# A weight cast placed by TensorE's progress in the piece three ahead

## The chip, the cores and the metric

The kernel runs on one core of a Trainium2 chip. The metric is the device time of one execution in microseconds (us). The core's engines work side by side, each through its own list of instructions in order, and wait for one another by semaphores: TensorE (PE) multiplies, VectorE (DVE) and ScalarE (ACT) work element by element, GpSimd (POOL) helps with a few, and SyncE (SP) issues the fetches of weights.

## What is computed

Two layers of a decoder trunk, on 272 positions (16 learned meta positions and a sequence of 256) and a model width of 1024, all in 32-bit floating point. The reference, cut to its frame:

```python
for l in range(DEPTH):
    h = rms_norm(x, norm1_g[l])
    u = h @ w_in[l]
    (u_conv, c_q, c_kv, k_rope, hq, hf, hi, hg, u_gate) = jnp.split(u, SPLIT_POINTS, axis=-1)
    y_a = conv_module(u_conv, ...)      # causal depthwise conv of 31 taps, layer norm, projection
    y_b = mla(c_q, c_kv, k_rope, ...)   # 8 heads of latent attention, causal softmax, projection
    y_c = hgrn2(hq, hf, hi, hg, ...)    # gated linear recurrence, 4 heads, projection
    gates = jax.nn.sigmoid(u_gate).reshape(B, L, N_BRANCH, D)
    mix = gates[:, :, 0] * y_a + gates[:, :, 1] * y_b + gates[:, :, 2] * y_c
    x = x + mix @ w_out[l]
    h2 = rms_norm(x, norm2_g[l])
    x = x + jnp.square(jax.nn.relu(h2 @ w_ff1[l])) @ w_ff2[l]
return x[:, N_META:]
```

## The kernel before

All activations lie with channels on the 128 partitions and positions along the row. The dense weights are cut into 276 pieces of 128 x 1024 numbers, and `piece` (L206) brings one in: `fetch` issues its DMA on SP into one of three buffers `wraw`, ACT casts it to the matmul type as `whi` (L211), and DVE subtracts this from the raw piece to get the remainder `wlo` (L213). `whi` and `wlo` have four buffers each, so a cast overwrites the piece four back and must wait until PE has read that. A product is made of three matmuls, `mm3` (L220): high by high (L221), low by high (L222) and high by low (L223). A piece feeds eight such triples, 24 matmuls, for one accumulator `acc` (or `hx`) in PSUM. There are two `acc` buffers; ACT or DVE copies the finished one out, which frees it.

A layer has a mixer part and a feed-forward part. In the mixer part a list `dense` (L1012) holds the tiles of `w_in` (`head_tile`, L400, whose results `take`, L410, copies out), the gates (`gate_tile`, L980) and the projections of the three branches (`merge_tile`, L986). Between these the loop at L1023 takes steps of four streams: latent projections, HGRN2, attention, conv. The first merge tile needs the output `ys` of attention, so whatever is left of attention then runs with no other dense work to place: this is called attention's tail below.

The names in the tail: `mx` is a product of queries and keys in PSUM, `pr` its exp (L652), which ACT scales by the row's sum (L658, and for the 16 meta positions as `pm`, L657); `pt` is `pr` transposed by PE (L671) and `pts` its copy (L681); `sm` is the product with the values (L694, L701), and `ybhi` its cast (L217), which the merge tiles multiply by. HGRN2's own tail stands there too: `at`, `atm` and `atx` (L849, L863, L869) are its masked score blocks, `vtok` and `vmeta` (L883, L885) its values, transposed by PE (L879, L881) and multiplied with (L899 to L907). Before that HGRN2 takes an Ln of its decay on ACT in two halves, `lf` (L744), DVE scans each (L746), and ACT takes exponentials `ep` and `en` (L773, L774). `sg` (L417) is a tanh of an accumulator, with the copy at L419 beside it. Where a function is not in ACT's loaded table, the program has an ACT_TABLE_LOAD ahead of it. The conv's taps are multiply-adds on DVE (`cacc`, L939), and PE takes its mean over channels afterwards (`mx`, L947).

The order of each engine's list is set before the run by a scheduler that plays the program through in modelled time: of the instructions that could start it takes the one of highest priority. `tc.high_priority(offset=AHEAD)` raises fetch, cast and subtraction of a piece by 500 places, and so they are placed about as soon as a buffer is free. Semaphores are then added where data need them.

Of the kernel before, what the change touches and what calls it, by code (L numbers as in the profile page):

```python
# [35 lines left out]
FF = 4 * D  # L36
KF = FF // P
AHEAD = 500
NGATE = 15
NLAT = 8  # L40
BRANCHES = (1, 2, 0)
# [45 lines left out]
def block_kernel(ctx, tc, xT_d, pp_d, cc_d, win_d, wuq_d, wukv_d, wbr_d, wout_d, wff1_d, wff2_d, out_d):  # L87
    nc = tc.nc
    pe, act, dve, pool = nc.tensor, nc.scalar, nc.vector, nc.gpsimd
# [14 lines left out]
    def fetch(src, n=1024):  # L104
        raw = wsp.tile([P, 1024], F32, name="wraw", tag="wraw")
        nc.sync.dma_start(out=raw[:, :n], in_=src[:, :n])
        return raw

    xT = resid.tile([P, KD, L], F32, name="xT")
    pp = const.tile([P, DEPTH, NPP], F32, name="pp")  # L110
    with tc.high_priority(offset=2 * AHEAD):
        nc.scalar.dma_start(out=pp, in_=pp_d)
# [88 lines left out]
    def psum_sm():  # L201
        return ps_sm.tile([P, 512], F32, name="sm", tag="sm")

    newest = {}

    def piece(src, raw=None):  # L206

        with tc.high_priority(offset=AHEAD):
            raw = raw or fetch(src)
            hi = wsp.tile([P, 1024], F32R, name="whi", tag="whi", bufs=4)  # L210
            act.copy(out=hi, in_=raw)  # L211
            lo = wsp.tile([P, 1024], F32R, name="wlo", tag="wlo", bufs=4)
            newest["lo"] = dve.tensor_tensor(out=lo, in0=raw, in1=hi.bitcast(F32), op=SUB).ins  # L213
        return hi, lo
# [3 lines left out]
        dve.tensor_tensor(out=lo, in0=src, in1=hi.bitcast(F32), op=SUB)  # L218

    def mm3(out, whi, wlo, xhi, xlo, start, stop):  # L220
        pe.matmul(out, whi, xhi, start=start, stop=False)  # L221
        pe.matmul(out, wlo, xhi, start=False, stop=False)  # L222
        pe.matmul(out, whi, xlo, start=False, stop=stop)  # L223

# [84 lines left out]
    for l in range(DEPTH):  # L309
# [25 lines left out]
        t4 = t4p.__enter__()  # L335
        gpool = tc.tile_pool(name=f"gates{l}", bufs=NGATE)
        gp = gpool.__enter__()
# [31 lines left out]
        def win_acc(j, n0):  # L369
            hi, lo = piece(win_d[l, j], first["kv"] if l == 0 and j == 1 else None)  # L370
            xh, xl = xg if j < NLAT else (hhi, hlo)
            ps = psum_hx() if j < NLAT and j % 2 == 0 else psum_acc()
            for k in range(KD):
                o = k * P
                mm3(ps[:, :L - n0], hi[:, o:o + P], lo[:, o:o + P], xh[:, k, n0:], xl[:, k, n0:],
                    k == 0, k == KD - 1)
            return ps
# [10 lines left out]
        def rope_keys(j):  # L388

            with tc.high_priority(offset=AHEAD):  # L390
                raw = first["kr"] if l == 0 else fetch(win_d[l, j], KD * ROPE)
# [57 lines left out]
        def latent_steps():  # L449
# [44 lines left out]
            for g in range(2):  # L494
                uqhi, uqlo = piece(wuq_d[l, g])
                for h in range(4):
                    ps = psum_mx()[:, :L]
                    for j in range(2):
                        o = j * 512 + h * P
                        mm3(ps, uqhi[:, o:o + P], uqlo[:, o:o + P], cqhi[:, j, :], cqlo[:, j, :], j == 0, j == 1)  # L500
                    act.activation(out=msq_[:QK, h, :], in_=ps[:QK], func=AF.Square)
                    dve.tensor_tensor(out=qT[g][:, h, :], in0=ps, in1=csg, op=MUL)
                    yield
                with together():
                    for h in (3, 2, 1, 0):
                        pe.matmul(sums[32 * h:32 * h + 32, :L], sel96[:QK, g, :], msq_[:QK, h, :], start=(g == 0), stop=(g == 1))
                yield
# [3 lines left out]
            for w in qtiles:  # L511
# [10 lines left out]
                                     in1=heads(ra[:, 1, q0:3]), op0=MUL, op1=MUL)  # L522

            ukhi, uklo = piece(wukv_d[l])
            kT = [unit(f"kT{g}") for g in range(2)]
            vv = [half(f"vv{w}", "vv", 3) for w in range(3)]
# [459 lines left out]
        def merge_tile(i):  # L986
            b, m = divmod(i, KD)
            yh, yl = ys[BRANCHES[b]]
            if i == 0:
                mix["sum"] = [unit(f"mix{j}") for j in range(2)]  # L990
            if i % 2 == 0:
                mix["w"] = piece(wbr_d[l, i // 2])
            bhi, blo = mix["w"]
            ps = (psum_acc, psum_hx, psum_hx)[b]()
            for k in range(4):
                o = (i % 2 * 4 + k) * P
                mm3(ps[:, :N], bhi[:, o:o + P], blo[:, o:o + P], yh[:, k, T0:], yl[:, k, T0:], k == 0, k == 3)
            g, total = gates[i], mix["sum"][m // 4][:, m % 4, :N]
            with tc.high_priority(offset=AHEAD):
                dve.scalar_tensor_tensor(out=total if b == 0 else g[:, :N], in0=g[:, :N], scalar=1.0, in1=ps[:, :N], op0=ADD, op1=MUL)  # L1000
            if b > 0:
                dve.tensor_tensor(out=total, in0=total, in1=g[:, :N], op=ADD)
            if b == 2:
                if m == 0:
                    mix["hi"] = actp.tile([P, KD, L], F32R, name="mhi", tag="ahi")
                    mix["lo"] = actp.tile([P, KD, L], F32R, name="mlo", tag="alo")
                act.activation(out=mix["hi"][:, m, T0:], in_=total, func=AF.Copy, scale=0.5)
                dve.scalar_tensor_tensor(out=mix["lo"][:, m, T0:], in0=total, scalar=0.5, in1=mix["hi"][:, m, T0:].bitcast(F32),
                                         op0=MUL, op1=SUB)


        dense = [(head_tile, j) for j in range(NLAT, N_HEAD_TILES)] + [(gate_tile, i) for i in range(NGATE)]  # L1012
        for i in range(3 * KD):
            dense.append((merge_tile, i))
            if i + NGATE < 3 * KD:
                dense.append((gate_tile, i + NGATE))
        head_index = {(t[0], t[1]): j - NLAT for j, t in enumerate(tiles)}
# [26 lines left out]
        xhi = actp.tile([P, KD, L], F32R, name="xhi", tag="ahi")  # L1044
# [165 lines left out]
```

## Time and profile before

| | us |
|---|---|
| median of 3 runs | 954.34 (954.14 to 955.79) |
| the profiled execution | 952.41 |
| its span in the trace | 950.6 |
| PE busy | 927.6 |
| DVE busy | 714.1 |
| ACT busy | 525.0 |
| POOL busy | 55.7 |

The trace is of the profiled execution. Its span runs from the first recorded instruction to the last, and 1.8 us of the execution lie around it. Busy time of an engine leaves out waits and the issue of DMAs. A matmul's end is modelled, so the distance between two starts tells more of PE than a duration. In a timeline an entry stands for one instruction or a few alike in a row (x2), and the square brackets hold the idle time of that engine just before it and what ended it.

### The profile page before, as it was taken

The page shows a single profiled execution, that of the slowest core. Times are in us where ns is not written, and L with a number is a line of the kernel's source. Part 1 is how long each engine was busy: PE and PEld are TensorE (multiplying, and loading weights), DVE is VectorE, ACT ScalarE, POOL GpSimd, SP SyncE. Part 2 cuts the span into 40 slices and gives each one's busy share as a digit, 9 for nine tenths or more (in the row PEclk, how much of TensorE's full clock was granted, in tenths as well). Part 3 has the DMA queues.
Part 4 walks back from the last instruction along what each step waited for, and adds up shares of the span by engine and source line. Part 5 has one row for each costly group of instructions (what it writes and reads, how often), then busy time and mean ns, then how long its engine had stood idle before and what let it go on. Part 6 is the DMA issues. An engine that isn't in the chain of part 4 may idle for free.

```text
span 950.6 us, 18626 instructions
## 1 busy us (share of the span) xinstructions
PE 927.6 (98%) x7474; PEld 892.0 (94%) x7474; DVE 714.1 (75%) x1348; ACT 525.0 (55%) x945; POOL 55.7 (6%) x87
## 2 busy tenths in 40 slices
PE   7999999899999999999999999999999999999998
PEld 5899999879999999999999889998799999999998
DVE  7789999986887766555557799999869886675552
ACT  7567665644546555544445587666345566654331
POOL 4004100011000000000010021000100000000000
PEclk9999999999999999999999999999999999999999
DMA  8454433324545655555545444344145565555651
GB/s 267 132 178 136 154 112 129 117 66 134 175 137 180 197 177 174 171 174 173 177 159 174 137 132 158 113 153 123 60 153 182 169 193 191 191 186 186 204 198 56
DMA packets 42422, 149.16 MB, mean 157 GB/s; under 512 B 4704, under 2 KB 6368, under 8 KB 42336
## 3 DMA queue, kind: packets, MB, share of 16 engines
q1 hardware_dynamic: 40608, 146.10, 47.9%
q10 hardware_dynamic: 1728, 1.88, 0.6%
q8 instruction: 58, 0.95, 0.4%
q14 instruction: 28, 0.23, 0.1%
HBM read 146.91 MB, written 1.05 MB: 156 GB/s over the span
## 4 chain that ended last, share of the span: by engine, by line
PE 90%; DVE 4%; ACT 3%; issue 2%; DMA 1%; SPq 0%; ACTq 0%
PE acc L221 18%; PE acc L222 17%; PE acc L223 17%; PE hx L221 9%; PE hx L223 9%; PE hx L222 9%; DVE wlo L213 2%; PE mx L636 1%; PE hx L812 1%; ACT whi L211 1%; PE sm L694 1%; DMA xT<-in_xT_dram 1%; PE pt L671 1%; PE sm L701 0%; PE mx L221 0%
## 5 line engine op out<-in xcount | busy, mean ns | idle before, releaser
L211 ACT CAST whi<-wraw 128x1024 fp32r<-128x1024 f32 x276 | 289.5, 1050 | 339.0 <-PE acc L223 182.2
L213 DVE TENSOR_TENSOR wlo<-wraw,whi 128x1024 fp32r<-128x1024 f32 x276 | 337.3, 1223 | 156.4 <-ACT whi L211 155.3
L221 PE MATMUL acc<-hhi,whi 128*128 128x272 f32 (+1 forms) x704 | 206.0, 293 | 2.6 <-ACT scrahi L419 1.9
L223 PE MATMUL acc<-hlo,whi 128*128 128x272 f32 (+1 forms) x704 | 202.6, 288 | 0.2 <-DVE hlo L218 0.2
L222 PE MATMUL acc<-hhi,wlo 128*128 128x272 f32 (+1 forms) x704 | 201.9, 287 | 0.0
L221 PEld LDWEIGHTS acc<-hhi,whi 128*128 128x128 f32 x704 | 132.6, 188 | 7.5 <-ACT scrahi L419 2.1
L223 PEld LDWEIGHTS acc<-hlo,whi 128*128 128x128 f32 x704 | 132.3, 188 | 2.0 <-DVE hlo L218 0.6
L222 PEld LDWEIGHTS acc<-hhi,wlo 128*128 128x128 f32 x704 | 132.7, 188 | 1.2 <-issue 0.4
L939 DVE SCALAR_TENSOR_TENSOR cacc<-hpad,pph,cacc 128x272 f32<-128x272 f32 (+1 forms) x240 | 111.7, 487 | 0.6
L222 PE MATMUL acc<-xhi,wlo 128*128 128x272 f32 (+1 forms) x256 | 73.4, 287 | 0.0
L222 PE MATMUL hx<-xhi,wlo 128*128 128x272 f32 (+1 forms) x256 | 73.2, 286 | 0.0
L223 PE MATMUL acc<-xlo,whi 128*128 128x272 f32 (+1 forms) x256 | 73.1, 286 | 0.0
L222 PE MATMUL hx<-fhi,wlo 128*128 128x272 f32 (+1 forms) x256 | 72.9, 285 | 0.0
L223 PE MATMUL hx<-xlo,whi 128*128 128x272 f32 (+1 forms) x256 | 72.9, 285 | 0.0
L222 PE MATMUL acc<-fhi,wlo 128*128 128x272 f32 (+1 forms) x256 | 72.9, 285 | 0.0
L221 PE MATMUL acc<-fhi,whi 128*128 128x272 f32 (+1 forms) x256 | 72.8, 284 | 0.0
L221 PE MATMUL hx<-fhi,whi 128*128 128x272 f32 (+1 forms) x256 | 72.8, 284 | 0.0
L223 PE MATMUL acc<-flo,whi 128*128 128x272 f32 (+1 forms) x256 | 72.7, 284 | 0.0
L223 PE MATMUL hx<-flo,whi 128*128 128x272 f32 (+1 forms) x256 | 72.7, 284 | 0.0
L221 PE MATMUL acc<-xhi,whi 128*128 128x272 f32 (+1 forms) x256 | 72.7, 284 | 0.0
L221 PE MATMUL hx<-xhi,whi 128*128 128x272 f32 (+1 forms) x256 | 72.7, 284 | 0.0
L223 PEld LDWEIGHTS acc<-xlo,whi 128*128 128x128 f32 x256 | 48.3, 189 | 0.1
(375 smaller groups left out, 2094.6 us busy)
## 6 DMA issues: line engine op xcount, KB each, us to landing
wraw<-in_wff_dram SPq DMA_DIRECT2D x128, 512.0 KB, 3.3
wraw<-in_win_dram SPq DMA_DIRECT2D x102, 512.0 KB, 3.4
wraw<-in_wbr_dram SPq DMA_DIRECT2D x24, 512.0 KB, 3.5
wraw<-in_wout_dram SPq DMA_DIRECT2D x16, 512.0 KB, 3.4
wraw<-in_wuq_dram SPq DMA_DIRECT2D x4, 512.0 KB, 3.4
xT<-in_xT_dram SPq DMA_DIRECT2D x4, 272.0 KB, 5.9
wraw<-in_wukv_dram SPq DMA_DIRECT2D x2, 512.0 KB, 3.8
out_dram<-xT ACTq DMA_DIRECT2D x8, 128.0 KB, 2.3
```

Of the source, the lines that this page charges most:

```text
L211: act.copy(out=hi, in_=raw)
L213: newest["lo"] = dve.tensor_tensor(out=lo, in0=raw, in1=hi.bitcast(F32), op=SUB).ins
L221: pe.matmul(out, whi, xhi, start=start, stop=False)
L222: pe.matmul(out, wlo, xhi, start=False, stop=False)
L223: pe.matmul(out, whi, xlo, start=False, stop=stop)
L636: pe.matmul(sh, qT[h // 4][:, h % 4, WIN[w]:WIN[w] + P], kT[h // 4][:, h % 4, :nk], start=(n == 1), stop=(j == 1))
L671: pe.transpose(by_key[:, h % 2, kw, :], pr[:, NM + kw * P:NM + (kw + 1) * P], ident)
L694: pe.matmul(place(po_of[w], h, P), vv[kw + 1][:, h * VD:(h + 1) * VD], by_key[:, j, kw, :], start=False, stop=False)
L812: pe.matmul(ps[:, w - 1, h, :], kl[:, h, WIN[w]:WIN[w] + P], ql[:, h, q0:q0 + 64], start=True, stop=True)
L939: dve.scalar_tensor_tensor(out=a, in0=hpad[:, c, T0 + k:T0 + k + N], scalar=hpar(l, "cw", c * CK + k), in1=a, op0=MUL, op1=ADD)
```

## The change

`mm3` now keeps the first matmul of each triple in a list, `dense_mms`. `piece` notes in `begun` how long that list is when the piece is made, and from the fourth piece on it gives the cast a dependence on a matmul: the fifth triple (INTO = 4) counted from where the piece three back (LAG = 3) was made. The dependence is of the kind NoSync: the scheduler must place the cast after that matmul in its modelled time, but no semaphore is made of it. Number and kind of instructions stay as they are, but for two loads of ACT's table. Line numbers of the changed kernel are higher by 1 at the cast and by 6 from `wlo` on.

```diff
--- before.py
+++ after.py
@@ -36,6 +36,7 @@
 FF = 4 * D
 KF = FF // P
 AHEAD = 500
+LAG, INTO = 3, 4
 NGATE = 15
 NLAT = 8
 BRANCHES = (1, 2, 0)
@@ -201,14 +202,19 @@
     def psum_sm():
         return ps_sm.tile([P, 512], F32, name="sm", tag="sm")
 
-    newest = {}
+    newest, dense_mms, begun = {}, [], []
 
     def piece(src, raw=None):
 
         with tc.high_priority(offset=AHEAD):
             raw = raw or fetch(src)
             hi = wsp.tile([P, 1024], F32R, name="whi", tag="whi", bufs=4)
-            act.copy(out=hi, in_=raw)
+            cast = act.copy(out=hi, in_=raw)
+
+            begun.append(len(dense_mms))
+            if len(begun) > LAG:
+                tc.add_manual_dep(cast.ins, dense_mms[begun[-1 - LAG] + INTO].name,
+                                  mybir.DependencyInfo(mybir.DependencyClass.NoSync, mybir.DependencyReason.DATA), reason="lead")
             lo = wsp.tile([P, 1024], F32R, name="wlo", tag="wlo", bufs=4)
             newest["lo"] = dve.tensor_tensor(out=lo, in0=raw, in1=hi.bitcast(F32), op=SUB).ins
         return hi, lo
@@ -218,7 +224,7 @@
         dve.tensor_tensor(out=lo, in0=src, in1=hi.bitcast(F32), op=SUB)
 
     def mm3(out, whi, wlo, xhi, xlo, start, stop):
-        pe.matmul(out, whi, xhi, start=start, stop=False)
+        dense_mms.append(pe.matmul(out, whi, xhi, start=start, stop=False).ins)
         pe.matmul(out, wlo, xhi, start=False, stop=False)
         pe.matmul(out, whi, xlo, start=False, stop=stop)
```

The scheduler's result differs on ACT above all. First, ACT in layer 0 at attention's tail; `acc_2566` is the last dense piece ahead of it, `whi_2753` the cast of a piece that is used after it. Before:

```order
L211 CAST whi_2700<-wraw_2698 128x1024 [waits DMAHW0_49,PE_49]
L984 ACTIVATE gate_2549<-acc_2524 128x272
L652 ACTIVATE pr_1780,mxs_1318<-mx_1773,mxs_1318,rq_890 128x272 [waits DVE_49]
L211 CAST whi_2753<-wraw_2751 128x1024 [waits DMAHW1_49,PE_49]
L984 ACTIVATE gate_2591<-acc_2566 128x272
L849 COPY at1_1143<-hx_2251 64x2x64 [waits PE_49]
L849 COPY at2_1144<-hx_2251 64x2x64
L863 COPY atm_1148<-hx_2336 16x256 [waits PE_49]
L863 COPY atm_1148<-hx_2336 16x256
L652 ACTIVATE pr_1793,mxs_1318<-mx_1787,mxs_1318,rq_890 128x272 [waits DVE_49]
L657 ACTIVATE pm_1320<-pr_1780,mxs_1318 128x16 [waits DVE_49]
L658 ACTIVATE pr_1780<-pr_1780,mxs_1318 128x256
```

After the change, the same place:

```order
L658 ACTIVATE pr_1780,mxs_1318<-mx_1773,mxs_1318,rq_890 128x272 [waits DVE_49]
L212 CAST whi_2700<-wraw_2698 128x1024 [waits DMAHW0_49,PE_49]
L990 ACTIVATE gate_2549<-acc_2524 128x272
L658 ACTIVATE pr_1793,mxs_1318<-mx_1787,mxs_1318,rq_890 128x272 [waits DVE_49]
L663 ACTIVATE pm_1320<-pr_1780,mxs_1318 128x16 [waits DVE_49]
L664 ACTIVATE pr_1780<-pr_1780,mxs_1318 128x256
L855 COPY at1_1143<-hx_2251 64x2x64 [waits PE_49]
L855 COPY at2_1144<-hx_2251 64x2x64
L869 COPY atm_1148<-hx_2336 16x256 [waits PE_49]
L869 COPY atm_1148<-hx_2336 16x256
L990 ACTIVATE gate_2591<-acc_2566 128x272 [waits PE_49]
L687 COPY pts_1858<-pt_1851 128x256 [waits PE_49]
```

and its end, nine rows on:

```order
L687 COPY pts_1924<-pt_1918 128x128 [waits PE_49]
L917 ACTIVATE on_2593<-hx_2555 16x512 [waits PE_49]
L223 CAST ybhi_1314<-sm_1700 128x4x128 [waits PE_49]
L212 CAST whi_2753<-wraw_2751 128x1024 [waits DMAHW1_49]
L212 CAST whi_2786<-wraw_2784 128x1024 [waits DMAHW2_49,PE_49]
```

The cast of `whi_2753` has moved from ahead of `gate_2591` to behind `ybhi_1314`, and the second exp and the scaling of `pr_1780` to ahead of `gate_2591`.

Second, ACT in layer 1 where HGRN2's decay is made; `sg_6795` and the copy behind it empty the accumulator `acc_6770`. Before:

```order
L417 ACT_TABLE_LOAD
L417 ACTIVATE sg_6713<-acc_6688 128x272
L419 COPY scrahi_6298<-acc_6688 128x272
L553 ACTIVATE kn_6735<-mx_6726,ra_6378 128x512 [waits DVE_49,Activation_49]
L744 ACT_TABLE_LOAD
L744 ACTIVATE lf_6843<-lf_6843 128x544 [waits DVE_49]
L572 ACTIVATE kT0_6641<-pt_6673,pp_86 128x4x16 [waits PE_49]
L557 ACTIVATE kq_6738<-kn_6735 128x512 [waits Activation_49]
L211 CAST whi_7058<-wraw_7056 128x1024 [waits DMAHW0_49,PE_49]
L417 ACT_TABLE_LOAD
L417 ACTIVATE sg_6795<-acc_6770 128x272
L419 COPY scrahi_6298<-acc_6770 128x272
```

After the change:

```order
L515 COPY qsum_6626<-sm_6402 128x272 [waits PE_49]
L750 ACTIVATE lf_6843<-lf_6843 128x544 [waits DVE_49]
L212 CAST whi_6930<-wraw_6928 128x1024 [waits DMAHW7_49,PE_49]
L423 ACT_TABLE_LOAD
L423 ACTIVATE sg_6713<-acc_6688 128x272
L425 COPY scrahi_6298<-acc_6688 128x272
L779 ACTIVATE ep_6976<-dd_6975 128x544 [waits DVE_49,Activation_49]
L780 ACTIVATE en_6977<-dd_6975 128x544 [waits DVE_49,Activation_49]
L559 ACTIVATE kn_6735<-mx_6726,ra_6378 128x512 [waits DVE_49]
L212 CAST whi_7058<-wraw_7056 128x1024 [waits DMAHW0_49,PE_49]
L423 ACTIVATE sg_6795<-acc_6770 128x272
L425 COPY scrahi_6298<-acc_6770 128x272
```

The first Ln, `lf_6838`, stands two rows ahead of both pieces; between it and `lf_6843` there is no tanh any more, and `ep_6976` and `en_6977` have moved ahead of `kn_6735`.

Third, ACT in layer 1 at attention's tail; `acc_8269` is the last dense piece ahead of it, and `whi_8449` the cast of a piece used after it. Before:

```order
L849 COPY at2_6964<-hx_8092 64x2x64
L652 ACTIVATE pr_7250,mxs_6890<-mx_7243,mxs_6890,rq_6630 128x272 [waits DVE_49]
L211 CAST whi_8449<-wraw_8447 128x1024 [waits DMAHW4_49,PE_49,Activation_49]
L863 COPY atm_6968<-hx_8177 16x256 [waits PE_49]
L863 COPY atm_6968<-hx_8177 16x256
L984 ACTIVATE gate_8294<-acc_8269 128x256
L652 ACTIVATE pr_7302,mxs_6890<-mx_7296,mxs_6890,rq_6630 128x272 [waits DVE_49]
L657 ACTIVATE pm_6892<-pr_7250,mxs_6890 128x16 [waits DVE_49]
L658 ACTIVATE pr_7250<-pr_7250,mxs_6890 128x256
```

After the change:

```order
L990 ACTIVATE gate_8258<-acc_8233 128x256
L658 ACTIVATE pr_7250,mxs_6890<-mx_7243,mxs_6890,rq_6630 128x272 [waits DVE_49]
L990 ACTIVATE gate_8294<-acc_8269 128x256 [waits PE_49]
L855 COPY at1_6963<-hx_8092 64x2x64 [waits PE_49]
L855 COPY at2_6964<-hx_8092 64x2x64
L869 COPY atm_6968<-hx_8177 16x256 [waits PE_49]
L869 COPY atm_6968<-hx_8177 16x256
L663 ACTIVATE pm_6892<-pr_7250,mxs_6890 128x16 [waits DVE_49]
L664 ACTIVATE pr_7250<-pr_7250,mxs_6890 128x256
L658 ACTIVATE pr_7302,mxs_6890<-mx_7296,mxs_6890,rq_6630 128x272 [waits DVE_49]
```

The cast of `whi_8449` is gone from here (it stands behind `ybhi_6887`, 13 rows on), `gate_8294` stands ahead of `at1_6963`, and the scaling of `pr_7250` ahead of the exp of `pr_7302`. On PE, the conv's channel mean `mx_8624` stands behind the piece of `acc_8557` before, and ahead of it after the change; the four matmuls of `sm_6402` within the piece of `acc_6483`, which stood as two, one and one, stand in one group.

## Rows read from the trace of the kernel before

**Rows 1.** The page's first part: busy time, share of the span and instructions, by engine.

```profile
PE 927.6 (98%) x7474; PEld 892.0 (94%) x7474; DVE 714.1 (75%) x1348; ACT 525.0 (55%) x945; POOL 55.7 (6%) x87
```

**Rows 2.** Busy time by stretch: length, engines with instructions, PE's granted clock, DMA.

```profile
180.00:190.00 10.00, 7.37 (x62) 6.55 (x59) 9.73 (x27) 7.09 (x18) 0.00 (x0) 1.00 0.33 107
...
400.00:410.00 10.00, 10.00 (x82) 10.00 (x81) 4.97 (x6) 4.53 (x6) 0.00 (x0) 1.00 0.57 179
...
590.00:600.00 10.00, 10.00 (x83) 9.50 (x82) 10.00 (x27) 5.44 (x10) 0.29 (x1) 1.00 0.33 106
...
660.00:670.00 10.00, 6.84 (x54) 4.36 (x53) 8.09 (x20) 6.85 (x19) 0.00 (x0) 1.00 0.35 107
```

**Rows 3.** Waits of PE: in total, times, the longest.

```profile
PE pt L671 <- ACT pr L658: 4.5, 3, 2.6
...
PE hx L221 <- DVE gate L1000: 0.8, 3, 0.4
```

**Rows 4.** Waits of ACT: in total, times, the longest.

```profile
ACT whi L211 <- PE acc L223: 182.2, 122, 4.1
```

**Rows 5.** The page's groups: busy, mean ns of one, idle before and what ended it.

```profile
L211 ACT CAST whi<-wraw 128x1024 fp32r<-128x1024 f32 x276 | 289.5, 1050 | 339.0 <-PE acc L223 182.2
...
L213 DVE TENSOR_TENSOR wlo<-wraw,whi 128x1024 fp32r<-128x1024 f32 x276 | 337.3, 1223 | 156.4 <-ACT whi L211 155.3
...
L939 DVE SCALAR_TENSOR_TENSOR cacc<-hpad,pph,cacc 128x272 f32<-128x272 f32 (+1 forms) x240 | 111.7, 487 | 0.6
```

**Rows 6.** Timeline of ACT, layer 0, attention's tail: start, us, instruction, idle before.

```profile
186.23 1.05 ACT L211 CAST whi<-wraw 128x1024 fp32r<-128x1024 f32 x1 [1.12 <-PE acc L223]
...
189.42 0.50 ACT L658 ACTIVATE pr<-pr,mxs 128x256 f32<-128x256 f32 x1
```

**Rows 7.** Timeline of PE, layer 0, attention's tail.

```profile
189.97 0.44 PE L671 MATMUL pt<-ident,pr 128*128 128x128 f32 x2 [2.63 <-ACT pr L658]
...
194.65 1.03 PE L899 MATMUL hx<-vmeta,at 128*16 128x512 f32 x2 [1.18 <-ACT vmeta L885]
...
198.34 0.39 PE L221 MATMUL acc<-ybhi,whi 128*128 128x272 f32 x1 [0.68 <-ACT ybhi L217]
```

**Rows 8.** Timeline of ACT, layer 1, HGRN2's decay.

```profile
553.49 1.28 ACT L744 ACT_TABLE_LOAD   x1
...
554.78 0.66 ACT L744 ACTIVATE lf<-lf 128x544 f32<-128x544 f32 x1
...
558.71 0.38 ACT L419 COPY scrahi<-acc 128x272 f32<-128x272 f32 x1
```

**Rows 9.** Timeline of PE, layer 1, the accumulator after it.

```profile
559.14 0.39 PE L221 MATMUL acc<-hhi,whi 128*128 128x272 f32 x1 [1.86 <-ACT scrahi L419]
```

**Rows 10.** Timeline of ACT, layer 1, attention's tail.

```profile
661.03 1.04 ACT L211 CAST whi<-wraw 128x1024 fp32r<-128x1024 f32 x1 [1.47 <-issue]
...
663.90 0.50 ACT L658 ACTIVATE pr<-pr,mxs 128x256 f32<-128x256 f32 x1
```

**Rows 11.** Timeline of PE, layer 1, attention's tail.

```profile
662.89 0.65 PE L879 MATMUL hx<-ident,scrahi 128*128 128x128 f32 x4 [0.76 <-ACT atm L863]
...
664.45 0.44 PE L671 MATMUL pt<-ident,pr 128*128 128x128 f32 x2 [0.90 <-ACT pr L658]
...
667.34 0.44 PE L671 MATMUL pt<-ident,pr 128*128 128x128 f32 x2 [0.94 <-ACT pr L658]
...
673.03 0.38 PE L221 MATMUL acc<-ybhi,whi 128*128 128x256 f32 x1 [0.68 <-ACT ybhi L217]
```

**Rows 12.** Timeline of PE, layer 0, normed input.

```profile
35.91 0.39 PE L221 MATMUL acc<-hhi,whi 128*128 128x272 f32 x1 [0.55 <-ACT qq L414]
```

**Rows 13.** Timeline of PE, layer 1, sums of squares of the query norm.

```profile
529.76 0.65 PE L506 MATMUL sm<-mla_sq,sel 96*32 96x272 f32 x2
```

**Rows 14.** Timeline of DVE, layer 1, the conv's last two taps.

```profile
690.15 1.00 DVE L939 SCALAR_TENSOR_TENSOR cacc<-hpad,pph,cacc 128x256 f32<-128x256 f32 x2
```

**Rows 15.** Timeline of PE, layer 1, the conv's channel mean.

```profile
694.33 0.64 PE L947 MATMUL mx<-cacc,selc 128*32 128x256 f32 x8
```

## The prediction

> **What bounds the kernel now.** Three views were read. The page's first part comes first: TensorE (PE) is busy for 98% of the span, VectorE (DVE) for three quarters and ScalarE (ACT) for a little over half [rows 1]. So only idle time of PE can be won, some 23 us, and a move of ACT work is worth what it takes out of that. Next, the busy time by stretch [rows 2]: in the feed-forward part PE has no idle time (400 to 410 us: 10.00 of 10, 82 matmuls, so 0.122 us from one to the next, and 24 x 0.122 = 2.9 us for a piece of weights). It is idle where attention ends and little dense work is left: 7.37 of 10 at 180 us in layer 0, 6.84 at 660 us in layer 1. Third, whom PE waits for [rows 3]: softmax results `pr` from ACT above all, 4.5 us in three waits. The whole answer holds no wait on `whi` or `wlo`, the cast weights themselves. The weights are early, then, and it is ACT's other results that are late.
>
> The view of ACT's waits says why they can be late: 182.2 us of its idle time stands in front of casts that wait until PE has read the buffer that they overwrite [rows 4]. ACT works in order, so what stands behind such a cast waits with it. The change lets the scheduler place a cast later in this order. It adds no wait on the chip: the dependence is known to the scheduler alone, and no engine has more instructions than before.
>
> **The change part by part.** The sum is made on the profiled execution of 952.41 us; the median of the three runs is 954.34, 1.93 above it, and the gain is then taken from the median. Casts and subtractions are as many as before and cost the same on their engines, 1.05 and 1.22 us each [rows 5]. What counts is what stands before what. The fetches on SP keep their order.
>
> *Layer 0, attention's tail.* The cast of `whi_2753` waits for the end of the last dense piece, runs at 186.23 us and keeps the exp of one head and the scaling of `pr_1780` behind it; the scaling runs at 189.42 [rows 6]. PE waits for it 2.63 us, then 1.18 for `vmeta` and 0.68 for `ybhi` [rows 7], 4.49 together. In the changed order the exp and the scaling stand ahead of `gate_2591`, and the cast stands behind the whole tail. Its piece is needed only some 72 matmuls after the tail, 72 x 0.122 = 8.8 us, against 1.05 + 1.22 = 2.3 us for cast and subtraction, so that cover holds. The first wait goes in full. Of the 1.18 about 0.5 stays: the four copies to `vmeta` still follow two copies of `vtok` and one of `pts`, and I add these by hand against the PE work beside them. The 0.68 stays, being the time that ACT needs for `ybhi` at the very end. Gain 4.49 - 0.5 - 0.7 = 3.3; bounds 0 and 4.5.
>
> *Layer 1, the decay of HGRN2.* ACT switches its function table four times between 547 and 558 us, since an Ln stands on either side of a tanh (the third load is shown). Each load is 1.28 us [rows 8]. PE then waits for the copy that runs at 558.71 and starts the next accumulator at 559.14, 1.86 us late [rows 9]. In the changed order the two Ln stand side by side, with one cast and one copy between them that need no table, and one load of each kind vanishes, 2 x 1.28 = 2.6 us of ACT. What is late next is DVE's scan of the first Ln, ahead of the second; added by hand it ends about 0.6 us before ACT is held up for long, and the copy comes about 0.3 us before PE wants the buffer. Gain 1.9, the whole wait; bounds 0 and 1.9. The Trainium skill, "ScalarE: Activation LUTs", section "What ACT_TABLE_LOAD costs", gives about 1283 ns for the load and about 1380 ns of drain, 2.66 us a switch. The rows agree with the load; they show no drain, for the Ln starts at 554.78, 0.01 us behind a load that began at 553.49. By the page ACT would gain 5.3 us and not 2.6; the sum is the same, because PE has only 1.9 to give.
>
> *Layer 1, attention's tail.* Likewise the cast at 661.03 stands before the scaling at 663.90 [rows 10], and PE waits 0.76, 0.90, 0.94, 0.68 [rows 11] and a fifth time 0.56, together 3.84. The cast moves behind the tail here too, but the attention steps now come one later with respect to the dense work, and `gate_8294`, which needs the end of the last dense piece, moves ahead of the scaling of `pr_7250`. Added by hand, about 1.6 us of waiting remains before the first `pt` and 1.2 later. Gain 3.84 - 2.8 = 1.0; bounds 0 and 1.8.
>
> *Small gains.* At 35.91 PE waits 0.55 for a copy of an accumulator behind a cast [rows 12]; the cast moves five casts back. DVE's norm chain is close behind, so 0.4 (0 to 0.55). The sums of squares of the query norm stand on PE as 2 + 1 + 1 between single matmuls that take about 0.3 us to the next start and not 0.122 [rows 13]; as one group they spare two such, 2 x 0.2 = 0.4 (0 to 0.4).
>
> *Losses.* At three places PE now uses an accumulator five matmuls after the piece whose gate or partial sum frees it; before, 13 to 29 matmuls lay between. The nearest row is PE's wait for `gate`, 0.8 in three and 0.4 at most [rows 3]: 0.2 each, 0.6 in all (0 to 1.2). And the conv branch of layer 1: its channel mean on PE, at 694.33 [rows 15], needs DVE's last tap, which ends at 691.15 [rows 14]; 3.2 us are spare. It now stands one dense piece earlier, 2.9 us, and the gains of layer 1 pull PE up by another 2.9 while DVE can follow with perhaps 1.5 of these. That leaves 3.2 - 2.9 - 2.9 + 1.5 = -1.1, a wait of about 1.0 (0 to 2.9).
>
> Sum: 3.3 + 1.9 + 1.0 + 0.4 + 0.4 = 7.0, less 0.6 and 1.0, a gain of 5.4 us: 947.0 in the profiled execution, 954.34 - 5.4 = **948.9** as a median. With every gain at its bound and no loss the gain is 9.15 us, 945.2.
>
> PE's clock was granted at 1.00, its 2.4 GHz level, through the stretches with these waits [rows 2], so a wait is counted at its own length. By the Trainium skill, "TensorE: Matmul & The Clock Gate", section "What's actually happening", idleness brings the clock down to half; a removed wait would then give back more than itself. No row here shows that lower level, and the sum doesn't count on it.
>
> **The rivals.** *First, layer 1 gives its gains back.* DVE is busy 10.00 of 10 us at 590 us [rows 2]. If it can't follow PE there, the 1.9 and the 1.0 turn into waits at the conv mean and at the merge. Then 3.3 + 0.4 + 0.4 - 0.6 - 1.0 = 2.5 are left, 951.8, and with the conv wait at its bound 0.6, 953.7. For it speaks that the attention step is one later; against it, that DVE was idle for 1.9 of the 10 us from 660 on [rows 2], which an earlier PE shortens.
>
> *Second, the change doesn't act on the chip.* No semaphore enforces the later cast, so ACT runs in its listed order as soon as it can. If the tail's waits come from the chains of softmax and HGRN2 themselves, all that shifts is in whose name ACT waits: 954.3. Against it: at 186.23 the cast stands ahead of an exp whose input, a product on PE, was done before the last dense piece began.
>
> *Third, slower: weights come too late.* A cast was placed once the piece four back was done, 72 matmuls ahead of its use; now it is placed from the middle of the piece three back, 60 matmuls ahead, 60 x 0.122 = 7.3 us. Cast and subtraction take 2.3, so 5.0 are spare. It is lost where the subtraction finds over 5.0 us of other work ahead of it on a full DVE, about ten taps of the conv at 0.49 [rows 5], and then PE waits for `wlo` by up to one such operation, 1.2 us a piece. About 47 pieces run from 550 to 690 us (140 / 2.9). From six of them on (6 x 1.2 = 7.2) the gain is used up and the kernel measurably slower; nine would give 954.34 - 5.4 + 10.8 = 959.7. Against it: the order shows the subtractions just as many matmuls ahead of their use in steady state as before, and PE waits for none of them now.
>
> **How the numbers follow.** A measurement of this kernel can tell about 0.2% from no change, that is below 952.4 or above 956.2. The forecast, 946.5 to 951.5, gets 0.64, since the rows name the waits and the order shows what stood before them; all gains at their bounds (below 946.5) 0.05; the first rival 0.16, spread from 951.8 to 953.7 and half of it below 952.4; the second 0.06; the third 0.09. Faster is then 0.64 + 0.05 + 0.08 = 0.77, the same 0.08 + 0.06 = 0.14, slower 0.09. A range of 945.2 to 953.6 leaves out about 0.02 below, and above the second and third rivals and the end of the first, 0.17.
>
> **What would show it.** Right: no wait for `pr` of 2.6 us in layer 0, and the first merge matmul about 3.3 us sooner after the last dense piece; seven table loads and not nine, and no wait of 1.9 us on `scrahi`; new short waits on `gate` and `mix`; a wait of about 1 us at the conv mean. Wrong: waits of PE on `wlo` or `whi`, which are the third rival; the same waits under other names, which are the second; a conv wait near 3 us or a tail in layer 1 as long as before, which are the first.

## The result and the profile after

The changed kernel takes 943.11 us (median; 942.67 to 943.95), the kernel before 954.28. The ratio is 0.988 (95% interval 0.9863 to 0.9898): 11.2 us faster, where 5.4 were forecast, and below the range of 945.2 to 953.6. Its profiled execution takes 943.10 us, with a span of 941.3.

The page's first part, as in [rows 1], and the whole answer on PE's waits (in total, times, the longest), as in [rows 3], of the kernel after:

```profile
PE 924.8 (98%) x7474; PEld 893.1 (95%) x7474; DVE 713.0 (76%) x1348; ACT 525.4 (56%) x943; POOL 56.1 (6%) x87
...
PE hx L403 <- DVE wkr L399: 7.3, 1, 7.3
PE pt L677 <- ACT pr L664: 1.6, 1, 1.6
PE acc L227 <- ACT ybhi L223: 1.3, 2, 0.7
PE acc L229 <- DVE hlo L224: 0.8, 1, 0.8
PE hx L907 <- ACT vmeta L891: 0.6, 1, 0.6
PE hx L905 <- ACT vmeta L891: 0.5, 1, 0.5
PE hx L927 <- DVE on L922: 0.2, 1, 0.2
```

The work is the same, with two table loads fewer on ACT (943 instructions for 945). One wait for `pr` is left of three, and the waits for `gate` [rows 3] and for the copy of an accumulator [rows 9] are gone. There is still no wait for the cast weights.

Layer 0's attention tail, as in [rows 6, 7]: first ACT, then PE, of the kernel after (start, us, instruction, idle before):

```profile
185.57 0.50 ACT L664 ACTIVATE pr<-pr,mxs 128x256 f32<-128x256 f32 x1
...
195.03 1.05 ACT L212 CAST whi<-wraw 128x1024 fp32r<-128x1024 f32 x1
```

```profile
187.93 0.38 PE L677 MATMUL pt<-ident,pr 128*128 128x128 f32 x2
...
192.39 1.03 PE L905 MATMUL hx<-vmeta,at 128*16 128x512 f32 x2 [0.54 <-ACT vmeta L891]
...
195.19 0.39 PE L227 MATMUL acc<-ybhi,whi 128*128 128x272 f32 x1 [0.68 <-ACT ybhi L223]
```

The scaling is done 1.9 us before PE wants it; the waits are 0, 0.54 and 0.68, against 0, 0.5 and 0.7 worked out. The cast stands at the end.

HGRN2's decay in layer 1, as in [rows 8]: ACT of the kernel after.

```profile
543.42 0.66 ACT L750 ACTIVATE lf<-lf 128x544 f32<-128x544 f32 x1 [0.66 <-DVE lf L748]
...
545.46 1.28 ACT L423 ACT_TABLE_LOAD   x1
...
550.22 0.40 ACT L425 COPY scrahi<-acc 128x272 f32<-128x272 f32 x1
```

The second Ln waits 0.66 us for DVE, whose scan of the first half the prediction had named as late next; one load follows, and the copy ends at 550.62; PE uses the buffer from 551.77 and doesn't wait. Layer 1's attention tail, as in [rows 11], the sums of squares, as in [rows 13], and the conv's last tap and channel mean, as in [rows 14, 15]:

```profile
655.98 0.44 PE L677 MATMUL pt<-ident,pr 128*128 128x128 f32 x2 [1.56 <-ACT pr L664]
...
661.10 1.12 PE L907 MATMUL hx<-vmeta,atm 128*128 128x512 f32 x2 [0.60 <-ACT vmeta L891]
...
665.79 0.39 PE L227 MATMUL acc<-ybhi,whi 128*128 128x256 f32 x1 [0.67 <-ACT ybhi L223]
```

```profile
527.12 0.67 PE L512 MATMUL sm<-mla_sq,sel 96*32 96x272 f32 x8
```

```profile
682.65 0.48 DVE L945 SCALAR_TENSOR_TENSOR cacc<-hpad,pph,cacc 128x256 f32<-128x256 f32 x1
...
683.72 0.64 PE L953 MATMUL mx<-cacc,selc 128*32 128x256 f32 x8
```

To see where the time went, PE's start at the same piece of work (a name with a number is one tile) is read in both traces, and in a second trace of the kernel before (the first experiment):

| PE starts | before | before, second trace | after | after less before |
|---|---|---|---|---|
| last dense piece ahead of layer 0's tail | 183.00 | 183.44 | 183.37 | +0.37 |
| first merge matmul of layer 0 | 198.34 | 201.90 | 195.19 | -3.15 |
| latent projections, layer 1 (`hx_6108`) | 494.25 | 497.79 | 490.81 | -3.44 |
| HGRN2's first scores, layer 1 (`hx_7465`) | 595.75 | 599.27 | 588.86 | -6.89 |
| last dense piece ahead of layer 1's tail | 657.15 | 660.67 | 650.30 | -6.85 |
| first merge matmul of layer 1 | 673.03 | 676.54 | 665.79 | -7.24 |
| last merge tile but two (`hx_9006`) | 727.01 | 730.46 | 717.94 | -9.07 |
| last matmul | 946.55 | 949.98 | 937.26 | -9.30 |

So the first trace accounts for 9.3 us: 3.5 in layer 0's tail, 3.45 between 490 and 596, 0.4 in layer 1's tail, 1.8 from there to `hx_9006`. The other 1.9 us lie between this trace's execution (952.41) and the median.

### The profile page after: what moved, and what is told of

Its sections match the earlier page's. It is cut to its first block, busy times and chain, and to the rows that moved or that the text cites. A ratio compares the mean times of both kernels' runs of the same rounds, so it can differ in the third digit from the quotient of the medians.

```text
span 941.3 us, 18610 instructions
## 1 busy us (share of the span) xinstructions
PE 924.8 (98%) x7474; PEld 893.1 (95%) x7474; DVE 713.0 (76%) x1348; ACT 525.4 (56%) x943; POOL 56.1 (6%) x87
## 4 chain that ended last, share of the span: by engine, by line
PE 94%; DVE 4%; ACT 1%; issue 0%; DMA 0%; POOL 0%
PE acc L227 18%; PE acc L229 18%; PE acc L228 18%; PE hx L227 10%; PE hx L229 10%; PE hx L228 10%; PE mx L642 1%; DVE cacc L945 1%; PE hx L818 1%; DVE wlo L219 1%; PE sm L700 1%; PE pt L577 1%; PE hx L403 0%; PE pt L677 0%; PE mx L227 0%
```

## The experiments

**The kernel before, once more.** No edit.

> The kernel before, unchanged, for a second trace of it. Its profiled execution took 952.41 us where the timed ones take 954.2, and the trace of the changed kernel accounts for 9.3 of the 11.2 us. If the 952.41 was one short execution (theory), this one takes 954 to 955 and its span is some 1.9 us longer than 950.6, spread over the start or over small waits. If profiled executions are always shorter than timed ones (rival), the profiled one here takes 952.4 again, and the 1.9 us are a matter of profiling.

954.14 (median of 8), its profiled execution 955.84, span 954.0: 3.4 us more than in the first trace. The table puts it in one place, layer 0's tail: 201.90 - 183.44 = 18.5 us against 15.3. Busy time by stretch (columns as in [rows 2]; the last but two is PE's granted clock), first trace, then second:

```profile
188.00:190.00 2.00, 0.03 (x1) 0.04 (x1) 1.73 (x4) 1.88 (x6) 0.00 (x0) 1.00 0.63 240
190.00:192.00 2.00, 2.00 (x18) 1.49 (x18) 2.00 (x6) 0.70 (x3) 0.00 (x0) 1.00 0.85 262
194.00:196.00 2.00, 1.35 (x5) 0.38 (x7) 0.05 (x1) 1.23 (x5) 0.00 (x0) 1.00 0.00 0
198.00:200.00 2.00, 1.67 (x13) 1.67 (x14) 2.00 (x6) 0.28 (x1) 0.83 (x1) 1.00 0.00 0
```

```profile
188.00:190.00 2.00, 0.00 (x0) 0.00 (x0) 1.73 (x5) 1.95 (x9) 0.00 (x0) 0.96 0.81 266
190.00:192.00 2.00, 1.59 (x10) 1.01 (x10) 2.00 (x6) 0.72 (x2) 0.00 (x0) 0.50 0.74 233
194.00:196.00 2.00, 2.00 (x15) 1.04 (x13) 0.47 (x2) 1.75 (x5) 0.00 (x0) 0.50 0.00 0
198.00:200.00 2.00, 2.00 (x10) 0.91 (x9) 0.67 (x2) 0.73 (x2) 0.00 (x0) 0.50 0.00 0
200.00:202.00 2.00, 1.32 (x11) 1.07 (x9) 1.58 (x6) 0.58 (x1) 1.19 (x1) 0.98 0.00 0
```

PE has the same gap of 2.63 us in both, from 187.3 to 190.0 in the first and from 187.8 to 190.4 in the second. In the second trace its clock falls to 0.50, the 1.2 GHz level, at the end of this gap, and is back at 1.00 by 201: everything between takes up to twice as long, and 3.1 us are lost. The clock had not been seen below 1.00 in the first trace. Over 25 executions of the kernel before in this job the time follows the mean clock (the granted clock averaged over an execution): 952.2 to 952.6 at 1.000, 953.9 to 954.4 at 0.998, 955.2 to 956.5 at 0.995, 957.5 and 957.7 at 0.992 (those at 0.996 lie between 953.5 and 956.1). The rival, that a profiled execution is always shorter, falls.

**Each layer by itself.** The edit to the changed kernel; for layer 1 alone the condition is `if len(begun) > 138:`.

```diff
-            if len(begun) > LAG:
+            if len(begun) > LAG and len(begun) <= 138:
```

> The dependence for the casts of layer 0 alone; the orders of layer 0 are those of the changed kernel, those of layer 1 those of the kernel before. Theory: each layer's gain is its own, read from the traces: 3.4 us at the end of attention in layer 0 and next to nothing elsewhere in it, so 954.3 - 3.4 = 950.9. Rival: a part of the gain is owed to both layers together (weights that are fetched ahead over the border of the layers): then this and the next kernel do not add up to 11.2.

> The dependence for the casts of layer 1 alone. Theory (gains by layer, read from the traces): 3.4 us between 490 and 565 us, 0.5 at the end of attention, 2.0 at the conv's end and the merge, together 5.9, so 948.4, and up to 1.9 us less if the difference between profiled and timed executions of the kernel before belongs to layer 1. Rival as above: the two layers' gains do not add up.

Layer 0 alone 950.27 (0.994, 0.9919 to 0.996), layer 1 alone 948.86 (0.9931, 0.9915 to 0.9948), against 954.87 of the kernel before in this job: 4.6 and 6.0 us, together 10.6, near the 11.2. The gains add up, within the spread. In the traces layer 0's tail is 11.82 us with its part of the change and 18.49 without (with the clock at 0.50 there), layer 1's stretch from 494 to 596 us the same 98.05 as in the changed kernel.

**The two Ln apart again.** In the changed kernel's layer 1 the second Ln must follow the first tanh (the core of the edit):

```diff
                     sig["ln"] = act.activation(out=lff, in_=lff, func=AF.Ln, scale=-1.0, bias=1.0)
+                if l == 1 and hp == 1:
+                    tc.add_manual_dep(sig["ln"].ins, sig["i"].name, ...)
```

> The changed kernel with one more dependence for the scheduler: in layer 1 the second Ln of HGRN2 must follow a tanh, so that ACT loads its table four times there, as in the kernel before. Theory: the two table loads that the change spares are what removed PE's wait of 1.9 us for a copy of an accumulator; the wait comes back, and the time is 943.1 + 1.9 = 945.0. Rival: the wait went because the cast ahead of the copy moved; then the time stays at 943.1 within 0.5.

945.25 (945.21 to 945.47): 2.1 us more than the changed kernel, as expected. ACT's timeline has three loads between the first Ln and the copy, and PE waits again (whole answer as above, its line on the copy):

```profile
546.04 1.28 ACT L423 ACT_TABLE_LOAD   x1
...
547.75 1.28 ACT L752 ACT_TABLE_LOAD   x1
...
549.99 1.28 ACT L784 ACT_TABLE_LOAD   x1
...
553.64 0.38 ACT L427 COPY scrahi<-acc 128x272 f32<-128x272 f32 x1
```

```profile
PE acc L227 <- ACT scrahi L427: 1.3, 1, 1.3
```

PE's way from `hx_6108` to `hx_7465` takes 99.85 us, 1.8 more than in the changed kernel (98.05) and 1.65 less than before (101.50). So 1.8 of the 3.45 us of this stretch belong to the table loads, and 1.65 do not.

**The two casts at the head, alone, and all but these.** The edit to the changed kernel; the numbers are those of the pieces.

```diff
-            if len(begun) > LAG:
+            if len(begun) - 1 in (48, 186):
```

and, for the second kernel, `if len(begun) > LAG and len(begun) - 1 not in (48, 186):`.

> The dependence for two casts alone, the one that waited at the head of ACT's list in each attention tail (pieces 48 and 186); all others as in the kernel before. Theory 1: this cast is what kept the scaling back, and without it layer 0's tail is 3.5 us shorter (and keeps its clock), so 949 to 950.5, layer 1's tail up to 1.6 shorter. Theory 2: the scaling came late because the attention's steps as a whole stood late on ACT, behind copies that wait for PE; then most of PE's wait of 2.6 us stays (the scaling still stands behind the copies at and atm), the gain is 1 us for the cast itself, and the time is 953 to 954.

> The dependence for all casts but these two. By theory 1 layer 0's tail is as long as in the kernel before and some 4 to 5 us of the gain are lost: 947 to 948. By theory 2 the scaling of layer 0's tail still stands ahead of the cast, PE doesn't wait for it, and what is lost is the cast's 1 us ahead of other copies, in each layer at most: 943 to 945.

The two alone: 951.47 against 955.64 of the kernel before in this job (0.9953, 0.9938 to 0.9969), 4.2 us less, which lies between the ranges of the two theories. All but these: 942.64 (942.27 to 942.82; 0.9868, 0.9846 to 0.989), no slower than the changed kernel. For the wait on the scaling in layer 0 theory 2 holds. PE in layer 0's tail, with the two casts alone (and in layer 1's tail, the last line), then with all others:

```profile
189.00 0.69 PE L677 MATMUL pt<-ident,pr 128*128 128x128 f32 x2 [2.13 <-ACT pr L664]
...
198.61 0.40 PE L227 MATMUL acc<-ybhi,whi 128*128 128x272 f32 x1 [0.68 <-ACT ybhi L223]
...
673.18 0.39 PE L227 MATMUL acc<-ybhi,whi 128*128 128x256 f32 x1 [0.68 <-ACT ybhi L223]
```

```profile
187.87 0.38 PE L677 MATMUL pt<-ident,pr 128*128 128x128 f32 x2
190.66 0.44 PE L677 MATMUL pt<-ident,pr 128*128 128x128 f32 x2 [0.74 <-ACT pr L664]
...
196.04 0.39 PE L227 MATMUL acc<-ybhi,whi 128*128 128x272 f32 x1 [0.68 <-ACT ybhi L223]
```

With the cast out of the way PE still waits 2.13 us of the 2.63, since the scaling stands behind copies that wait for PE. With the cast in its old place ahead of `gate_2591`, but all other casts moved, the scaling is ahead of both, and the first wait is gone. What removed it is the place of the attention's steps on ACT, which the other casts had set.

The two casts alone still give over a third of the gain, at an equal clock too: with them the executions at a mean clock of 1.000 take 948.4 and 948.5, those of the kernel before 952.2 to 952.6. Theory 1 has its part in layer 1: in the trace its tail takes 673.18 - 658.73 = 14.45 us against 15.87 before, and PE's way from there to `hx_9006` 52.75 against 53.98. With all casts but these moved, the two take 14.8 and 52.05, so in these traces either half of the change was enough in layer 1.

**The conv's channel mean put back.** Its four matmuls must follow the dense piece of `acc_8557`:

```diff
-                        pe.matmul(part[32 * c:32 * c + 32, :N], selc, src[:, c, :N], start=True, stop=True)
+                        m = pe.matmul(part[32 * c:32 * c + 32, :N], selc, src[:, c, :N], start=True, stop=True)
+                        if l == 1 and src is acc:
+                            tc.add_manual_dep(m.ins, dense_mms[-5].name, ...)
```

> The changed kernel with the conv's channel mean of layer 1 put back behind the next dense piece on PE, as in the kernel before. Theory: standing earlier it let the conv's last steps on DVE finish earlier, which removed PE's two waits for gate at 725 and 727 us and what lies around them, about 1.2 us; they come back, and the time is 944.3. Rival: those waits went for another reason (PE's lead over DVE); then the time stays within 0.4 of 943.1.

943.35 (942.32 to 943.95), 0.24 above the changed kernel and within its spread, as the rival has it. PE has no wait for `gate` in this trace either, so the mean's place is not what removed these waits. It may still be worth a part: from the first merge matmul to `hx_9006` PE takes 718.87 - 665.89 = 52.98 us here, 0.8 more than in the changed kernel (52.15) and 1.0 less than before (53.98). The medians can't settle this, since four of the five executions here have a mean clock of 1.000 and those of the changed kernel 0.997 or 0.998; the one at 0.997 took 943.95.

**PE kept busy in the gap.** The kernel before, with transposes of the identity ahead of those that wait, placed behind the last product ahead of the gap (14, then 22; shown are the lines that add them, not the dependence that places them):

```diff
                 by_key = pt[:, :2 * w * P].rearrange("p (h w t) -> p h w t", h=2, w=w)
+                if l == 0 and w == 2 and hs[0] == NH - 2:
+                    for _ in range(FILL):
+                        fill.append(pe.transpose(by_key[:, 0, 0, :], ident, ident).ins)
```

> The kernel before with 14 transposes of the identity on PE in the gap of layer 0's attention tail, written to the PSUM tile that the next transposes overwrite; the order is otherwise that of the kernel before, and the wait for the scaling stays. Theory (clock): where an execution of the kernel before takes 954 us or more, PE's granted clock fell to 0.50 behind this gap (in the second trace from 190 to 200 us, 3.1 us lost) or in layer 1's tail. With PE kept busy it stays at 1.00 in layer 0: the tail there takes 15.3 us from the start of the last dense piece to the first merge matmul, as in the first trace and not 18.5 as in the second; no execution has a mean clock below 0.996, and the median is 1 to 2 us below that of the kernel before. Rival: the clock falls for another reason (the ten us ahead, or the chip as a whole); then executions at 0.992 to 0.995 come as often as before and the median stays at 954.9.

> As the kernel with the filled gap, with 22 transposes in place of 14, since 14 took 1.75 us and left 0.95 of the 2.63 us idle. Theory (clock): with no idle time of more than about 1.2 us left in layer 0's tail, PE's clock stays at 1.00 there in all executions, so none has a mean clock below 0.997 (a fall in layer 1's tail alone gives 0.998), and the median is 952.3 to 954.2 where the kernel before has 955. Rival: executions at 0.992 to 0.996 come in the same share as with the kernel before.

With 14 of them, 954.47 against 955.64 in the same job (0.9992, 0.9976 to 1.0008): 3 of 12 executions have a mean clock of 0.996 or less, against 15 of 23 of the kernel before, but two of these three are at 0.993, so the strict form of the expectation fails, and the gain is not clear of noise. With 22, 952.91 against 955.86 (0.9976, 0.9966 to 0.9987): none of 12 is below 0.998, and 7 are at 1.000, where the kernel before has 11 of 17 at 0.996 or less and none at 1.000. PE with 22 (timeline, then the clock by stretch):

```profile
188.67 2.62 PE L672 MATMUL pt<-ident 128*128 128x128 f32 x22
191.37 0.44 PE L675 MATMUL pt<-ident,pr 128*128 128x128 f32 x2
...
196.05 1.03 PE L907 MATMUL hx<-vmeta,at 128*16 128x512 f32 x2 [1.18 <-ACT vmeta L893]
```

```profile
188.00:190.00 2.00, 2.00 (x20) 1.51 (x18) 2.00 (x7) 1.98 (x6) 0.00 (x0) 1.00 0.46 121
190.00:192.00 2.00, 1.92 (x18) 1.52 (x18) 1.73 (x5) 1.45 (x6) 0.00 (x0) 1.00 0.60 201
194.00:196.00 2.00, 0.86 (x12) 0.33 (x10) 1.44 (x4) 1.96 (x7) 0.00 (x0) 1.00 0.00 0
...
560.00:562.00 2.00, 1.49 (x6) 1.49 (x7) 2.00 (x6) 2.00 (x5) 0.00 (x0) 0.59 0.53 150
```

The added matmuls compute nothing, the scaling comes no sooner, and the kernel is still 2.9 us faster on the median (1.2 to 3.3 by the interval). That is about what the clock's fall behind this gap costs the kernel before. The five executions at 0.998 take 954.1 to 955.3, and the traced one, 955.28, shows one reason: its clock is at 1.00 through layer 0's tail, but down at 560 us, behind PE's wait for the accumulator's copy [rows 9], 1.85 us here. From `hx_6108` to `hx_7465` it takes 598.56 - 495.63 = 102.93 us, 1.4 more than the first trace (101.50). So this wait, too, can cost more than its length.

**The same in the changed kernel's layer 1.** The edit is that of the last two, in layer 1 of the changed kernel with 8 transposes.

> The changed kernel with 8 transposes of the identity on PE in the remaining gap of layer 1's tail (1.56 us), where its own trace shows the clock at 0.50 for some 3 us. Theory: the clock stays up there, layer 1's tail takes 14.3 us from the start of the last dense piece to the first merge matmul and not 15.5, and the median falls by up to 1.2 us, to 942 or a little above. Rival: the clock falls for the other gaps of this tail too, then 943.1.

943.25 (942.83 to 943.65), no gain. The changed kernel's own trace has the clock down in this tail:

```profile
656.00:658.00 2.00, 2.00 (x17) 1.66 (x18) 2.00 (x7) 1.20 (x5) 0.00 (x0) 0.89 0.42 168
658.00:660.00 2.00, 2.00 (x16) 1.21 (x15) 2.00 (x6) 1.79 (x6) 0.00 (x0) 0.50 0.00 0
660.00:662.00 2.00, 1.40 (x4) 0.58 (x4) 2.00 (x6) 1.38 (x5) 0.00 (x0) 0.76 0.00 0
```

The filled kernel's executions have a mean clock of 0.999 and 1.000, yet the time is the same within its spread. From the tail's first product on PE to the first merge matmul its trace has 665.19 - 653.04 = 12.15 us, against 665.79 - 653.20 = 12.59 here, 0.4 of the 1.2 expected: PE's wait for `vmeta` in this tail is 1.2 us where it was 0.60. The faster matmuls wait longer for ACT, so a part of the clock's fall had been hidden. The 14.3 us expected for the tail had come from the trace with the two Ln apart, where other waits stand in it (0.46, 0.20, 0.97, 0.49, 0.68) and 1.13 us of waiting follow. Nor is the run clean: the scheduler also placed the conv's channel mean one dense piece later, as in the kernel with the mean put back.

```profile
685.94 0.64 PE L961 MATMUL mx<-cacc,selc 128*32 128x256 f32 x8
```

From the first merge matmul to `hx_9006` the filled kernel takes 717.91 - 665.19 = 52.72 us against 52.15, which takes the 0.4 back. What the fallen clock costs here by itself is open.

**Later still.** `LAG, INTO = 3, 7` and `2, 4`.

> The changed kernel with the cast placed after the last triple of the piece three back and not its fifth, 48 matmuls ahead of its use. Theory: on the chip a later cast still starts as soon as ACT reaches it, and PE has 48 x 0.122 = 5.9 us to spare against 2.3 for cast and subtraction; no wait on the weights, the gain depends on how the scheduler happens to order the tails, 942 to 946. Rival (weights too late): waits of PE on wlo where DVE is full, from 550 to 690 us, and over 946.

> The cast placed in the middle of the piece two back, 36 matmuls or 4.4 us ahead of its use, of which cast and subtraction take 2.3. Theory: 2.1 us are left for what stands ahead of them on ACT and DVE, which is too little where DVE is full; PE waits on wlo there, by up to 1.2 us a piece, and the time is above 943.1 by some us, 945 to 960. Rival: waits of PE on the weights don't appear, and the time is 943 or less.

947.5 (0.991, 0.9897 to 0.9923) and 950.96 (0.9949, 0.9936 to 0.9962). Both are slower than the changed kernel. The first misses the 942 to 946 expected, but not for the rival's reason: its matmuls on dense weights wait for no `whi` or `wlo`. It loses 3.65 of its 4.4 us in layer 0's tail (197.99 - 182.52 = 15.47 us against 11.82), where PE waits 1.97 us for DVE's `k` and the clock falls. In the second PE waits for weights, in three places (lines of the answer on PE's waits):

```profile
PE pt L677 <- ACT pr L664: 3.0, 2, 2.7
PE acc L227 <- ACT scrahi L425: 1.6, 1, 1.6
...
PE acc L228 <- DVE wlo L219: 0.7, 1, 0.7
PE mx L228 <- DVE wlo L219: 0.6, 1, 0.6
...
PE mx L227 <- ACT whi L212: 0.2, 1, 0.2
```

These are 1.5 us of the 7.8 that it loses. The larger waits are the old ones, for `pr` and for the copy: a later cast does not by itself put ACT's other work in a better place.

## Why the prediction was wrong

The direction and the mechanism held: the casts never came late, what stood behind them came sooner, no gain was hidden. The size failed, at 11.2 us against 5.4, and by these steps:

| term | forecast | measured, first trace |
|---|---|---|
| layer 0's tail | 3.3 | 3.5 |
| HGRN2's decay, layer 1 | 1.9 | 1.8 |
| layer 1's tail | 1.0 | 0.4, with the clock down |
| accumulator's copy at 36 us | 0.4 | about 0 |
| sums of squares, and more in that stretch | 0.4 | 1.65 |
| short leads of gate and partial sums | -0.6 | about 0 |
| conv mean and merge, layer 1 | -1.0 | +1.8 |
| first trace against the median | 0 | 1.9 |

- *The step from one execution to the median* failed. I took the gain of the trace from the median, as if both executions differed by the same 1.93 us with and without the change. These 1.93 us are the clock: the first trace was one of the few executions in which it stayed up behind the gap of 2.63 us. I counted this wait at its own length because no row showed the lower level. Layer 0's tail gave 3.5 us against that execution, and 18.49 - 11.82 = 6.7 us against one where the clock falls in it. The clock can fall behind the wait of 1.86 us in layer 1 as well, for 1.4 us more. The Trainium skill ("TensorE: Matmul & The Clock Gate", "What's actually happening") has an idle PE drop to its lower clock. The second trace agrees, with 0.50 behind the gap, but what this makes of a removed wait stood outside the sum. A spread that the numbers showed, 952.41 against 954.14 to 955.79, had asked for a cause.
- *The conv's term* failed, by its sign: 2.8 us. I let DVE follow PE by 1.5 of 2.9 us. Its last tap ends at 683.13, 8.0 us sooner than in the first trace and with 0.6 to spare before the mean. In layer 1's tail, from the last dense piece to the first merge matmul, DVE is idle for 1.2 us and not 2.9: most of its idle time there was waiting for PE, and went with it. I saw that an earlier PE shortens it [rows 2], in a rival, and didn't put it in the sum. Nor did I ask what PE's waits for `gate` in the merge [rows 3] would do once DVE was less behind: they went, and PE's way from the first merge matmul to `hx_9006` is 1.8 us shorter. Two waits of 0.39 and 0.21 are 0.6 of this. With the mean put back no such wait returns, though 0.8 us of the 1.8 do in that trace; how the rest came about is open.
- *The sums of squares* were mis-sized. They and the three products between them took from 528.86 [rows 13 shows the second of the groups] to 531.24, 2.4 us; in one group they start at 527.12 and the next matmul follows at 527.72, 0.60 us, and the three products are 0.4 more. That is 1.4, not 0.4: each small group had cost at its start and its end. That is read from the traces; it would cover most of the 1.65 us that the experiment with the two Ln leaves over, but was not tried by itself.
- *Layer 1's tail* was mis-sized, and the clock has a part in it again. The waits that stay in it are 1.56, 0.60 and 0.67, together 2.8 as worked out, but it gave 0.4 us and not 1.0, with the clock down in a part of it. With the gap filled and the clock up (the run with 8 transposes) it takes 665.19 - 650.14 = 15.05 us, against 665.79 - 650.30 = 15.49 here and 673.03 - 657.15 = 15.88 before: 0.8 us less.
- *The losses at short leads* of 0.6 us, a term of the sum, did not come; no wait for `gate` or `mix` is in the answer on PE's waits. *The copy at 36 us* was saved and 0.8 us for `hlo` took its place, as the norm chain on DVE close behind it had suggested.
- *The reason given for layer 0's tail* was half wrong though the number was right: I named the cast at 186.23. With it and its like in layer 1 alone moved, 2.13 us of the wait stay; with all others moved, it goes. The size came out right because it was read from the order as a whole.
- *The rivals.* The first is refuted: layer 1 kept its gains (6.0 us by itself). The second is refuted. The third begins to show at a lag of two pieces, with 1.5 us of waits for `wlo` and `whi`, and is no part of a lag of three. (Its 140 / 2.9 is 48 pieces and not 47; nothing hangs on that.)

## What to carry to other kernels

When an in-order engine serves a saturated one, a prefetch placed as soon as its buffer is free can push back the small work that the saturated engine needs next; give the scheduler a later bound for the prefetch, and judge it by the whole order that results, since the one instruction at the head may not be what counts. Ask of every gap of PE what the clock does behind it, in more than one execution: where times scatter, compare their mean clock before a gain is read off one trace. And where an engine is idle for want of the one that you make faster, let it follow in the sum.

## What the runs showed of the hardware

The same program with the same gap of 2.63 us on PE keeps its clock at the 2.4 GHz level in some executions and drops to the 1.2 GHz level in others (first and second trace). Where it drops behind this gap, in the second trace, it is down from 190 to 200 us, a stretch in which PE works in short groups, and 3.1 us are lost. A gap of 1.85 us between dense matmuls was followed by the same fall in the trace with 22 transposes, for 1.4 us. Matmuls that compute nothing, put into the first gap, kept the clock at 1.00 through the tail that was traced; no execution of 12 had a mean clock below 0.998, and the kernel before became faster by 2.9 us on the median. In layer 1's tail the same cure shortened the tail by 0.4 us while PE's wait for `vmeta` grew from 0.60 to 1.2, and the median did not move.
